# A two-layer hybrid encoder on one core: the second sequence's input normalised and transposed during the first one's attention, and the output projections with a tile of their own for the next layer's norm

## The chip, the core and the metric

One core of a Trainium2 chip. It has the engines PE (TensorE, matrix multiply and transpose), DVE (VectorE), ACT (ScalarE) and POOL (GpSimd); SP (SyncE) issues the DMAs of this kernel. Each engine executes its own instructions in the order in which the program gives them, and waits for the others through semaphores. The metric is device time in microseconds, lower is better.

## The reference, cut

Two sequences of 1024 tokens with 1024 features (`x_prompt` and `x_sample`) go through the same two layers. Layer 0 is attention (dilated windows and grouped queries), layer 1 is mean pooling over windows.

```python
h = _rmsnorm(x, pre_norm[l]) * (1.0 + scl) + shift   # shift, scl, gate: from c, by ada_w
if l % 2 == 0:
    m = _attn_mixer(h, attn_w_in[i], attn_q_norm[i], attn_k_norm[i], attn_w_out[i])
else:
    m = _pool_mixer(h, pool_w_in[i], pool_w_grp[i], pool_scale[i], pool_w_out[i])
x = x + gate * _rmsnorm(m, post_norm[l])
# in both mixers: (something of h @ w_in) * silu(gate part of h @ w_in), then @ w_out
```

## The kernel before, in words

Everything is fp32. A product is made of three matmuls: each operand is split into a high part and a low part that TensorE takes as fp32r, and high x high, high x low and low x high are added in PSUM. So three lines, such as L945 to L947, belong to one product.

`run` executes the stages for sequence s = 0 (prompt) and s = 1 (sample) in this order, with their places in the profiled span: `start` and `layer0(0)` (input and attention of the prompt, 0 to 800 us), `outproj0(0)` (output projection of layer 0, residual, and the norm of layer 1, 800 to 977), `layer0(1)` (to 1643), `outproj0(1)` (to 1798), `layer1(1)` (pooling layer of the sample, to about 2070), `layer1(0)` (to the end). The Python code writes instructions out in an order that interleaves generators by hand (`next(...)`), and a scheduler with a timeline of its own turns that into one fixed order for each engine. Tiles come from pools with so many buffers for each tag; an allocation waits until the oldest user of its buffer is done.

The places that the change touches:

- `outproj0`: eight tiles of 128 tokens. Tile i: `load(i)` brings the residual input `xt` (512 KB), PE makes the sums `S` (for the first two tiles they are made ahead of the stage, `pre`), ACT squares them for the post norm (L1061), POOL makes the reciprocal root (`rstd`, L123 to L125), DVE multiplies by the gate row (L1063) and adds the residual (L1064) in place in `xt`, and SP stores `xt` as x1 (`x_d<-xt`). Then `h_tile` makes the input of layer 1: ACT Square (L250), DVE scaling (L252) in place in `xt`, shift added by POOL (L253, for the last two tiles by DVE), eight PE transposes (L258), evacuation by ACT (L263) and, for the low part, DVE (L265). For s = 1 it goes to `hN`, in SBUF; for s = 0 to a stash in DRAM (`hs_d`), since layer 1 of the prompt is last.
- `outproj0(0)` does more: through the same `h_tile` it makes the layer-0 input of the second sequence from its raw input `xo` (`load_o`), tile by tile. `hq` is the queue of such generators, and `run_h` takes the next step of the oldest.
- `layer0`: attention. `adv(ui)` takes a step of unit ui of the input projection; for s = 0 and ui in 2, 3, 4 a part of the modulation (`ada_rest`) is made between such steps, at the steps listed in `marks`.
- `layer1(0)` begins by loading the stash and splitting it into high and low (L1083, L1084).
- `start` makes the layer-0 input of the first sequence in another form: scaling by the reciprocal root (L1299), transposes (L1304), and then scale and shift as an affine with a scalar for each partition (L1310 on ACT, L1311 on DVE), and the low part (L1312).

```python
            nc.vector.scalar_tensor_tensor(xt[i], jk, r, xt[i], op0=ALU.mult, op1=ALU.add)
            nc.sync.dma_start(x1o[i], xt[i])
            put = self.put_stash(op, i) if s == 0 else self.put_hT(hN, i)
            hq.append(self.h_tile(op, xt[i], g1, sh1, perm, put, jk, nc.vector if i >= NT - 2 else None))
```

The last line reuses `xt[i]`, which the store of the line before still reads.

Of the kernel before, what the change touches and what calls it, by code (L numbers as in the profile page):

```python
# [59 lines left out]
class Trunk:  # L60
    def __init__(self, ctx, tc, t):
# [28 lines left out]
        self.hs_d = self.dram.tile([NT, 2, P, 4, P], F32, name="hs_d")  # L90
# [73 lines left out]
    def ada_first(self, ap, stage):  # L164
# [4 lines left out]
        col = self.col = self.apool.tile([P, 2, 2, KT], F32, name="col")  # L169
# [75 lines left out]
    def h_tile(self, pool, x, g, sh, idm, put, junk=None, eng=None):  # L245
        nc = self.nc
        ss = pool.tile([P, 1], F32, name=self.n("ss"), tag="ss", bufs=6)
        if junk is None:
            junk = pool.tile([P, D], F32, name=self.n("jk"), tag="jk", bufs=2)
        nc.scalar.activation(junk, x, AF.Square, accum_out=ss)  # L250
        r = self.rstd(pool, ss, D, 1)
        nc.vector.scalar_tensor_tensor(x, x, r, g, op0=ALU.mult, op1=ALU.mult)  # L252
        (eng or nc.gpsimd).tensor_tensor(x, x, sh, ALU.add)  # L253
        for b in range(2):
# [6 lines left out]
            hi, lo, done = put(b)  # L261
            Tv = T.rearrange("p (k c) -> p k c", k=4)
            nc.scalar.activation(hi, Tv, AF.Copy)  # L263
            if lo is not None:
                nc.vector.tensor_tensor(lo, Tv, hi.bitcast(F32), ALU.subtract)  # L265
            if done:
                done()
            yield

    @staticmethod  # L270
    def put_hT(hT, i):
        def put(b):
            c = slice(i * P, (i + 1) * P)
            return hT[:, 4 * b : 4 * b + 4, 0, c], hT[:, 4 * b : 4 * b + 4, 1, c], None

        return put

    def put_stash(self, pool, i):
        def put(b):
            hl = pool.tile([P, 4, P], F32, name=self.n("hl"), tag="hl", bufs=2)  # L280
            return hl, None, lambda: self.nc.sync.dma_start(self.hs_d[i, b], hl)

        return put

# [288 lines left out]
    def layer0(self, s, hT, ap, side, after_proj, open2, run_h, first=None):  # L573
# [66 lines left out]
        rest = self.ada_rest(ap) if s == 0 else None  # L640
        started = {0, 1, 2}
# [3 lines left out]
        def adv(ui):  # L645
# [7 lines left out]
            if rest and ui in (2, 3, 4):  # L653
                if k in marks:
                    rest(k != marks[-1])
            if k == marks[-1] and ui + 1 < len(gens) and ui + 1 not in started:
                started.add(ui + 1)
                next(gens[ui + 1])
# [336 lines left out]
    def outproj0(self, s, wo, op, hN, pre, prefetch):  # L995
        nc, t = self.nc, self.t
        xsrc = (t["xp"] if s == 0 else t["xs"]).rearrange("(t m r) d -> t r m d", m=32, r=4)
        xos = t["xs"].rearrange("(hf p r) d -> r hf p d", hf=2, r=4)
        x1o = self.x1_d[s].rearrange("(t m r) d -> t r m d", m=32, r=4)
        hq = []  # L1000
        ys, xt, xo = {}, {}, {}

        def load(i):
            if i < NT:
                xt[i] = op.tile([P, D], F32, name=self.n("xt"), tag="xt", bufs=2)
                nc.sync.dma_start(xt[i], xsrc[i])
                if i >= 4:
                    ys[i] = []
# [539 lines left out]
```

## Time and profile before

| | |
|---|---|
| median of 3 runs | 2378.58 us (2374.77 to 2379.84) |
| the profiled execution: its span | 2374.5 us; no other time of that execution is given |
| PE busy | 2152.6 us, 91% |
| DVE busy | 1569.9 us, 66% |
| ACT busy | 1062.9 us, 45% |
| POOL busy | 1026.7 us, 43% |
| mean granted clock of TensorE | 0.957 |

The profile is of one execution, and its span lies within the three runs. Busy shares are averages over stages that differ; matmuls are pipelined, so a busy PE need not be at its peak. The granted clock is given as a share of full speed, 2.4 GHz; at the lower level, 1.2 GHz, a matmul takes twice the time.

### The profile page before, as it was taken

What the parts mean: (1) busy time and instruction counts of PE and PEld (TensorE: products, weight loads), DVE (VectorE), ACT (ScalarE), POOL (GpSimd) and SP (SyncE); (2) the same over time, 40 slices, a digit from 0 to 9 for tenths busy, and PEclk for the clock granted to TensorE, in tenths of its full rate; (3) what the DMA queues carried; (4) which work ended last, traced back from release to release, by engine and by line L of the source; (5) the groups of instructions that cost most, each with busy time, mean ns of one, the idle gap of its engine ahead of it and who ended that gap; (6) DMA issues with size and microseconds to landing.
All of it is one profiled execution on the core that took longest, in us unless ns stands there. A gap on an engine that the chain in (4) does not pass through costs nothing.

```text
span 2374.5 us, 38597 instructions
## 1 busy us (share of the span) xinstructions
PE 2152.6 (91%) x13777; PEld 1907.4 (80%) x13777; DVE 1569.9 (66%) x3453; ACT 1062.9 (45%) x2451; POOL 1026.7 (43%) x1455
## 2 busy tenths in 40 slices
PE   5999899999997866899999999988678999999998
PEld 3988788899997655898898999987457888778887
DVE  7788887767778344677878767775344454693536
ACT  6355555766665333355657666664221111310112
POOL 3675663135344253553321234433223345483552
PEclk9999999999997887999999999989789999999999
DMA  6123222112113444210011112124222111441113
GB/s 253 41 65 95 79 86 69 35 54 71 54 47 106 128 134 131 79 37 17 19 34 37 42 57 69 50 82 116 90 73 85 44 45 53 151 164 40 55 44 146
DMA packets 146561, 182.84 MB, mean 77 GB/s; under 512 B 13944, under 2 KB 109280, under 8 KB 146368
## 3 DMA queue, kind: packets, MB, share of 16 engines
q1 hardware_dynamic: 146032, 179.91, 24.1%
q8 instruction: 109, 1.79, 0.3%
q14 instruction: 84, 0.69, 0.1%
q10 hardware_dynamic: 144, 0.26, 0.0%
q0 software_dynamic: 192, 0.20, 0.0%
HBM read 142.33 MB, written 37.99 MB: 76 GB/s over the span
## 4 chain that ended last, share of the span: by engine, by line
PE 53%; DMA 15%; DVE 15%; issue 7%; POOL 6%; ACT 4%; SPq 0%; POOLq 0%; DVEq 0%; ACTq 0%
PE J L355 5%; PE J L357 5%; PE J L356 5%; PE S L1091 4%; PE S L1093 4%; PE S L1092 4%; DMA x_d<-xt 3%; PE H L676 3%; DMA xt<-xp 3%; POOL w L291 3%; PE T L714 2%; DVE E L694 2%; PE S L1186 2%; PE S L1188 2%; PE S L1187 2%
## 5 line engine op out<-in xcount | busy, mean ns | idle before, releaser
L291 POOL TENSOR_TENSOR w<-ws,w 128x256 fp32r<-128x256 f32 (+1 forms) x418 | 391.0, 949 | 360.0 <-DVE w L290 267.1
L355 PE MATMUL J<-w,hT 128*128 128x256 f32 x1664 | 482.5, 290 | 3.2 <-ACT xj L368 2.3
L357 PE MATMUL J<-w,hT 128*128 128x256 f32 x1664 | 477.5, 287 | 4.1 <-DVE hT L1312 3.9
L356 PE MATMUL J<-w,hT 128*128 128x256 f32 x1664 | 477.7, 287 | 0.4 <-POOL w L291 0.4
L355 PEld LDWEIGHTS J<-w,hT 128*128 128x128 f32 x1664 | 318.7, 192 | 7.2 <-ACT xj L368 3.7
L357 PEld LDWEIGHTS J<-w,hT 128*128 128x128 f32 x1664 | 318.5, 192 | 6.8 <-DVE hT L1312 4.6
L356 PEld LDWEIGHTS J<-w,hT 128*128 128x128 f32 x1664 | 318.5, 191 | 2.9 <-POOL w L291 0.9
L693 ACT ACTIVATE E<-T 128x512 fp32r<-128x512 f32 x384 | 226.8, 598 | 207.4 <-PE T L714 67.3
L694 DVE TENSOR_TENSOR E<-T,E 128x512 fp32r<-128x512 f32 x384 | 261.6, 682 | 84.5 <-ACT E L693 82.3
L290 DVE CAST w<-ws 128x256 fp32r<-128x256 f32 (+1 forms) x420 | 196.6, 493 | 169.5 <-PE S L1093 86.0
L683 ACT ACTIVATE P<-H,mx 128x512 f32<-128x512 f32 x256 | 173.7, 685 | 109.9 <-DVE mx L678 95.2
L1093 PE MATMUL S<-hT,w 128*128 128x512 f32 x512 | 200.5, 392 | 2.0 <-POOL w L291 2.0
L1091 PE MATMUL S<-hT,w 128*128 128x512 f32 x512 | 200.7, 392 | 0.0
L1092 PE MATMUL S<-hT,w 128*128 128x512 f32 x512 | 200.3, 391 | 0.0
L677 DVE TENSOR_REDUCE mx<-H 128x1 f32<-128x512 f32 x256 | 173.7, 681 | 34.1 <-PE H L676 32.0
L714 PE MATMUL T<-identr,P 128*128 128x128 f32 x1024 | 162.6, 274 | 6.9 <-DVE mr L151 3.2
L727 PE MATMUL O<-E,v 128*128 128x256 f32 x512 | 142.8, 301 | 14.1 <-DVE E L694 13.5
L793 ACT ACTIVATE P<-H,nm 128x256 f32<-128x256 f32 x256 | 117.7, 474 | 81.2 <-DVE nm L787 81.0
L726 PE MATMUL O<-E,v 128*128 128x256 f32 x512 | 146.1, 294 | 3.9 <-DVE X L748 2.2
L714 PEld LDWEIGHTS T<-identr,P 128*128 128x128 f32 x1024 | 122.4, 141 | 23.9 <-DVE mr L151 3.4
L441 POOL TENSOR_TENSOR hl<-xj,hl 128x256 fp32r<-128x256 f32 x64 | 48.2, 756 | 206.6 <-DVE hl L440 149.5
L727 PEld LDWEIGHTS O<-E,v 128*128 128x128 f32 x512 | 96.8, 189 | 27.2 <-DVE E L694 24.5
(264 smaller groups left out, 5228.8 us busy)
## 6 DMA issues: line engine op xcount, KB each, us to landing
ws<-win SPq DMA_DIRECT2D x192, 128.0 KB
ws<-ada_w SPq DMA_DIRECT2D x128, 128.0 KB
ws<-pwin SPq DMA_DIRECT2D x60, 256.0 KB
vb<-v_d SPq DMA_DIRECT2D x64, 144.0 KB
xt<-xp SPq DMA_DIRECT2D x16, 512.0 KB
ada<-ada_w SPq DMA_DIRECT2D x16, 512.0 KB
y_d<-X SPq DMA_DIRECT2D x32, 256.0 KB
v_d<-v SPq DMA_DIRECT2D x64, 128.0 KB
```

The costliest lines, as they stand in the source:

```text
L290: nc.vector.tensor_copy(hi, src)
L291: (nc.vector if dve_lo else nc.gpsimd).tensor_tensor(lo, src, hi.bitcast(F32), ALU.subtract)
L355: nc.tensor.matmul(ps, hi, w[:, 0, k, :], start=(k == 0), stop=False)
L356: nc.tensor.matmul(ps, hi, w[:, 1, k, :], start=False, stop=False)
L357: nc.tensor.matmul(ps, lo, w[:, 0, k, :], start=False, stop=(k == KT - 1))
L693: nc.scalar.activation(ov[0], Tv, AF.Copy)
L694: nc.vector.tensor_tensor(ov[1], Tv, ov[0].bitcast(F32), ALU.subtract)
L714: nc.tensor.transpose(T[:, (2 * e + i) * P : (2 * e + i + 1) * P], Pt[(h, 2 * g + i)][:, (2 * kp + e) * P : (2 * kp + e + 1) * P], self.ident)
L727: nc.tensor.matmul(O, st["v"][:, kk, :], pairs(ex, 1, e), start=False, stop=(kk == 7))
L1091: nc.tensor.matmul(ps[:, cs], w[:, 0, k, ws], hT[:, k, 0, cs], start=(k == 0), stop=False)
L1092: nc.tensor.matmul(ps[:, cs], w[:, 0, k, ws], hT[:, k, 1, cs], start=False, stop=False)
L1093: nc.tensor.matmul(ps[:, cs], w[:, 1, k, ws], hT[:, k, 0, cs], start=False, stop=(k == KT - 1))
```

## The change

The second sequence's layer-0 input is no longer made in `outproj0(0)`. A generator `x_ahead`, stepped in `layer0(0)` at the steps of units 2, 3 and 4 that are not marks, takes its eight raw tiles: load, Square and scaling by the reciprocal root, transposes, and a store of the transposed tile to a new DRAM tensor `xn_d`. In `outproj0(0)` a generator `h_affine` loads that by blocks of 128 features, and applies scale and shift as an affine. The stash `hs_d` of the first sequence likewise holds only the scaled and transposed tile, and `layer1(0)` applies its affine, with columns gathered from `mod_d`. In both `outproj0` the norm of the next layer is written into a tile of its own, `hx`, its transposes are put a tile later (`late`), and buffer counts change: `xt` 2 to 3, `jk` 1 to 2, `yh` 2 to 4, `y0` 2 to 3 for s = 0; the weight blocks fetched ahead for s = 1 have 2 buffers instead of 3. `h_tile` is divided into `normed` and `turned`.

```diff
         self.nc.sync.dma_start(r, self.mod_d[l, s, c : c + 1, :].to_broadcast([P, D]))
         return r
 
-    def h_tile(self, pool, x, g, sh, idm, put, junk=None, eng=None):
+    def normed(self, pool, x, out, junk, g=None, sh=None, eng=None):
         nc = self.nc
         ss = pool.tile([P, 1], F32, name=self.n("ss"), tag="ss", bufs=6)
-        if junk is None:
-            junk = pool.tile([P, D], F32, name=self.n("jk"), tag="jk", bufs=2)
         nc.scalar.activation(junk, x, AF.Square, accum_out=ss)
         r = self.rstd(pool, ss, D, 1)
-        nc.vector.scalar_tensor_tensor(x, x, r, g, op0=ALU.mult, op1=ALU.mult)
-        (eng or nc.gpsimd).tensor_tensor(x, x, sh, ALU.add)
+        if g is None:
+            nc.vector.tensor_scalar_mul(out, x, r)
+        else:
+            nc.vector.scalar_tensor_tensor(out, x, r, g, op0=ALU.mult, op1=ALU.mult)
+            (eng or nc.gpsimd).tensor_tensor(out, out, sh, ALU.add)
+
+    def turned(self, x, idm, put):
+        nc = self.nc
         for b in range(2):
             T = self.ptile("T")
             for k in range(4):
...
         E = ap.tile([P, 2 * ZB + 1, P], F32R, name=self.n("E"), tag="E", bufs=1)
         nc.gpsimd.memset(E[:, ZB, :].bitcast(F32), 0.0)
         rest = self.ada_rest(ap) if s == 0 else None
+        ahead = self.x_ahead(ap) if s == 0 else None
         started = {0, 1, 2}
         stepped = {}
         marks = [max(1, NSTEP * (i + 1) // 9) for i in range(7)]
...
             if rest and ui in (2, 3, 4):
                 if k in marks:
                     rest(k != marks[-1])
+                else:
+                    next(ahead, None)
+                    if k == NSTEP:
+                        next(ahead, None)
             if k == marks[-1] and ui + 1 < len(gens) and ui + 1 not in started:
                 started.add(ui + 1)
                 next(gens[ui + 1])
...
     def outproj0(self, s, wo, op, hN, pre, prefetch):
         nc, t = self.nc, self.t
         xsrc = (t["xp"] if s == 0 else t["xs"]).rearrange("(t m r) d -> t r m d", m=32, r=4)
-        xos = t["xs"].rearrange("(hf p r) d -> r hf p d", hf=2, r=4)
         x1o = self.x1_d[s].rearrange("(t m r) d -> t r m d", m=32, r=4)
-        hq = []
-        ys, xt, xo = {}, {}, {}
+        hq, late = [], []
+        ys, xt = {}, {}
 
         def load(i):
             if i < NT:
-                xt[i] = op.tile([P, D], F32, name=self.n("xt"), tag="xt", bufs=2)
+                xt[i] = op.tile([P, D], F32, name=self.n("xt"), tag="xt", bufs=3)
                 nc.sync.dma_start(xt[i], xsrc[i])
-                if i >= 4:
-                    ys[i] = []
-                    for f in range(2):
-                        y0 = op.tile([P, 4, P], F32, name=self.n("y0"), tag="y0", bufs=2)
-                        ys[i].append(op.tile([P, 2, 4, P], F32R, name=self.n("yh"), tag="yh", bufs=2))
-                        self.load_y(s, i, y0, ys[i][f], 4 * f, 4 * f + 4, 0)
-
-        def load_o(i):
-            if s == 0 and i < NT:
-                xo[i] = op.tile([P, D], F32, name=self.n("xo"), tag="xo", bufs=2)
-                nc.sync.dma_start(xo[i], xos[i // 2, i % 2])
+
+        def load_ys(i):
+            if 4 <= i < NT:
+                ys[i] = []
+                for f in range(2):
+                    y0 = op.tile([P, 4, P], F32, name=self.n("y0"), tag="y0", bufs=3 - s)
+                    ys[i].append(op.tile([P, 2, 4, P], F32R, name=self.n("yh"), tag="yh", bufs=4))
+                    self.load_y(s, i, y0, ys[i][f], 4 * f, 4 * f + 4, 0)
 
         def run_h(c):
             for _ in range(c):
...
                         run_h(1)
                         if i >= 4:
                             next(pf, None)
-            if s == 0:
-                jx = op.tile([P, D], F32, name=self.n("jx"), tag="jx", bufs=1)
-                hq.append(self.h_tile(op, xo[i], g0, sh0, self.ident, self.put_hT(hN, i), jx))
+            hq += late
+            hx = op.tile([P, D], F32, name=self.n("hx"), tag="hx", bufs=2)
             ss = op.tile([P, 1], F32, name=self.n("ss"), tag="ss", bufs=6)
-            jk = op.tile([P, D], F32, name=self.n("jk"), tag="jk", bufs=1)
-            nc.scalar.activation(jk, ps, AF.Square, accum_out=ss)
+            jk = op.tile([P, D], F32, name=self.n("jk"), tag="jk", bufs=2)
+            nc.scalar.activation(hx, ps, AF.Square, accum_out=ss)
+            nc.vector.tensor_tensor(jk, ps, pg, ALU.mult)
             r = self.rstd(op, ss, D, 1)
-            nc.vector.tensor_tensor(jk, ps, pg, ALU.mult)
             nc.vector.scalar_tensor_tensor(xt[i], jk, r, xt[i], op0=ALU.mult, op1=ALU.add)
             nc.sync.dma_start(x1o[i], xt[i])
-            put = self.put_stash(op, i) if s == 0 else self.put_hT(hN, i)
-            hq.append(self.h_tile(op, xt[i], g1, sh1, perm, put, jk, nc.vector if i >= NT - 2 else None))
+            self.normed(op, xt[i], hx, jk, g1, sh1, nc.vector if i >= NT - 2 else None)
+            put = self.put_stash(op, i, self.hs_d) if s == 0 else self.put_hT(hN, i)
+            late = [self.turned(hx, perm, put)]
+            if hN_of:
+                for _ in range(2):
+                    next(hN_of, None)
+        hq += late
         for _ in pf:
             pass
         return run_h
...
         kvw, self.kvw = self.kvw, None
         wu0 = kvw or self.l1_block(wp, t["pwin"][0])
         if s == 0:
-            for i in range(NT):
-                h = lp.tile([P, 2, 4, P], F32, name=self.n("h"), tag=("sg1", "wa")[i % 2], bufs=2)
-                for b in range(2):
-                    nc.sync.dma_start(h[:, b], self.hs_d[i, b])
-                    hi, lo = (hT[:, 4 * b : 4 * b + 4, e, i * P : i * P + P] for e in range(2))
-                    nc.scalar.activation(hi, h[:, b], AF.Copy)
-                    (nc.gpsimd if b and i % 2 else nc.vector).tensor_tensor(lo, h[:, b], hi.bitcast(F32), ALU.subtract)
+            hc = lp.tile([P, 2, KT], F32, name=self.n("hc"))
+            nc.sync.dma_start(hc, self.mod_d[1, 0, 0:2].rearrange("c (k p) -> p c k", p=P))
+            for _ in self.h_affine(lp, hT, self.hs_d, hc, ("sg1", "wa"), 2, 2):
+                pass
         outap = t["yp"] if s == 0 else t["ys"]
 
         def lin_c(ps, w, ct, c):
...
             def prefetch(sp):
                 self.wi = 0
                 out = []
-                yield from self.block_gen(None, sp, t["pwin"][0] if s else t["win"][8], out=out, bufs=1 if s == 0 else 3)
+                yield from self.block_gen(None, sp, t["pwin"][0] if s else t["win"][8], out=out, bufs=1 + s)
                 self.kvw = out[0]
 
             run_h = self.outproj0(s, after.wo, op, hT, pre, prefetch)
```

What the scheduler makes of it, at three places. First ACT, in the attention of the first sequence, around the Square of the third tile of `x_ahead`. `E` are evacuated transposes of the exponentials, `P` the exponentials (from scores `H` and maxima `mx`), `X` an evacuated output; `xa` is the raw tile, `xe` the tile that takes the squares and later the transposed halves. Before:

```order
L683 ACTIVATE P_2442,den_1925<-H_2432,mx_2434 128x512
L683 ACTIVATE P_2442,den_1925<-H_2433,mx_2434 128x512
L747 ACTIVATE X_2462<-O_2231 64x512
L693 ACTIVATE E_1302<-T_2471 128x2x256
L693 ACTIVATE E_1302<-T_2529 128x2x256
L683 ACTIVATE P_2526,den_1925<-H_2516,mx_2518 128x512
L683 ACTIVATE P_2526,den_1925<-H_2517,mx_2518 128x512
```

And with the change:

```order
L727 ACTIVATE P_2491,den_1950<-H_2481,mx_2483 128x512
L727 ACTIVATE P_2491,den_1950<-H_2482,mx_2483 128x512
L737 ACTIVATE E_1303<-T_2494 128x2x256
L791 ACTIVATE X_2511<-O_2266 64x512
L737 ACTIVATE E_1303<-T_2520 128x2x256
L249 ACTIVATE xe_2610,ss_2611<-xa_2560 128x1024
L737 ACTIVATE E_1303<-T_2580 128x2x256
L727 ACTIVATE P_2577,den_1950<-H_2567,mx_2569 128x512
L727 ACTIVATE P_2577,den_1950<-H_2568,mx_2569 128x512
```

The Square stands between the evacuation that follows `X` and the next one; the rest is as before.

Then SP, the queue that issues that tile's load. `ws` are blocks of weights, from the input projection (`win`) or the modulation (`ada_w`). Before:

```order
L306 DMA ws_2302<-win 128x256
L306 DMA ws_2306<-win 128x256
L306 DMA ws_2310<-win 128x256
L306 DMA ws_2314<-win 128x256
L306 DMA ws_2318<-win 128x256
L306 DMA ws_2322<-win 128x256
L157 DMA mod_d<-mr_2144 2x256
```

With the change:

```order
L345 DMA ws_2337<-win 128x256
L345 DMA ws_2341<-win 128x256
L285 DMA xn_d<-xe_2258 128x4x128
L345 DMA ws_2345<-win 128x256
L345 DMA ws_2349<-win 128x256
L294 DMA xa_2560<-xs 128x1024
L345 DMA ws_2353<-win 128x256
L345 DMA ws_2357<-win 128x256
L285 DMA xn_d<-xe_2258 128x4x128
L158 DMA mod_d<-mr_2171 2x256
```

The load of the tile and the two stores of the tile ahead of it stand among the weight loads, the load behind the fourth of them.

Last DVE, at the start of `outproj0(0)`. `row` are gate, scale and shift rows, `rr` reciprocal roots; `xo` is the raw input of the second sequence, `xk` a block of `xn_d`, `hT` the input that layer 0 of the second sequence reads. Before:

```order
L1063 TENSOR_TENSOR jk_10752<-S_10437,row_10729 128x1024
L1064 SCALAR_TENSOR_TENSOR xt_10731<-jk_10752,rr_10756,xt_10731 128x1024
L252 SCALAR_TENSOR_TENSOR xo_10735<-xo_10735,rr_10767,row_10737 128x1024
L1063 TENSOR_TENSOR jk_10811<-S_10603,row_10729 128x1024
L1064 SCALAR_TENSOR_TENSOR xt_10733<-jk_10811,rr_10815,xt_10733 128x1024
L252 SCALAR_TENSOR_TENSOR xo_10748<-xo_10748,rr_10841,row_10737 128x1024
L252 SCALAR_TENSOR_TENSOR xt_10731<-xt_10731,rr_10789,row_10743 128x1024
```

With the change:

```order
L1102 TENSOR_TENSOR jk_10939<-S_10630,row_10922 128x1024
L1104 SCALAR_TENSOR_TENSOR xt_10924<-jk_10939,rr_10944,xt_10924 128x1024
L252 TENSOR_SCALAR hx_10937<-xt_10924,rr_10952 128x1024
L1102 TENSOR_TENSOR jk_10969<-S_10796,row_10922 128x1024
L320 TENSOR_SCALAR xk_10929<-xk_10929,col 128x1024
L1104 SCALAR_TENSOR_TENSOR xt_10926<-jk_10969,rr_10974,xt_10926 128x1024
L320 TENSOR_SCALAR xk_10931<-xk_10931,col 128x1024
L321 TENSOR_TENSOR hT_10916<-xk_10929,hT_10916 128x1024
L320 TENSOR_SCALAR xk_10933<-xk_10933,col 128x1024
L282 COPY hl_11035<-T_11030 128x512
L321 TENSOR_TENSOR hT_10916<-xk_10933,hT_10916 128x1024
L320 TENSOR_SCALAR xk_10955<-xk_10955,col 128x1024
```

The scaling of the first tile (`hx`) now follows its multiply-add at once; the affines (L320) and low parts (L321) stand ahead of the scaling of the second tile, `L252 hx_10967`, which is the next row.

## Rows read from the trace of the kernel before

**Rows 1.** The page: its first line and the busy times.

```profile
span 2374.5 us, 38597 instructions
PE 2152.6 (91%) x13777; PEld 1907.4 (80%) x13777; DVE 1569.9 (66%) x3453; ACT 1062.9 (45%) x2451; POOL 1026.7 (43%) x1455
```

**Rows 2.** Windows: length, busy (instructions) of PE, PEld, DVE, ACT, POOL, clock, DMA, GB/s.

```profile
800.00:850.00 50.00, 38.73 (x167) 30.81 (x166) 17.66 (x20) 12.98 (x26) 20.63 (x21) 0.90 0.58 173
...
900.00:950.00 50.00, 31.35 (x130) 24.42 (x128) 21.25 (x21) 13.87 (x26) 20.70 (x24) 0.81 0.44 137
...
1700.00:1750.00 50.00, 33.47 (x123) 25.83 (x122) 22.99 (x26) 10.02 (x20) 19.50 (x23) 0.80 0.27 85
...
2050.00:2100.00 50.00, 49.35 (x214) 39.83 (x213) 47.08 (x36) 20.73 (x34) 37.80 (x31) 1.00 0.57 204
```

**Rows 3.** Waits, 800 to 975: total us, times, longest us.

```profile
DVE xt L252 <- DMA x_d<-xt: 51.4, 8, 8.6
...
ACT jx L250 <- DMA xo<-xs: 42.1, 5, 16.6
...
DVE xt L1064 <- DMA xt<-xp: 21.1, 5, 6.9
```

**Rows 4.** Waits, 1640 to 1800.

```profile
DVE xt L252 <- DMA x_d<-xt: 57.4, 8, 9.4
```

**Rows 5.** Chain that ended last, 780 to 1010: start us, us, what.

```profile
800.01 13.37 DMA xt<-xp
...
915.20 11.01 DMA x_d<-xt
...
976.91 0.44 PE T L258 x4
```

**Rows 6.** Chain that ended last, 1640 to 1800.

```profile
1644.40 17.83 DMA xt<-xs
...
1663.55 9.96 DMA x_d<-xt
...
1677.30 1.98 PE T L258 x8
1679.34 8.74 DMA xt<-xs
...
1798.15 1.05 PE S L1091 x2
```

**Rows 7.** Groups by line and shape, 800 to 975: busy us, mean ns | idle before.

```profile
L263 ACT ACTIVATE hl<-T 128x512 f32<-128x512 f32 x15 | 8.5, 591 | 22.0 <-PE T L258 21.1 <-ACT jk L250 0.9
...
L250 ACT ACTIVATE jx<-xo 128x1024 f32<-128x1024 f32 x8 | 8.4, 1053 | 42.1 <-DMA xo<-xs 42.1
```

**Rows 8.** Windows of 50 us in the first attention.

```profile
250.00:300.00 50.00, 43.35 (x304) 36.66 (x303) 46.11 (x106) 27.85 (x63) 33.01 (x49) 1.00 0.27 80
```

**Rows 9.** Timeline of ACT: start us, us, what, [idle before <-releaser].

```profile
200.47 0.60 ACT L693 ACTIVATE E<-T 128x512 fp32r<-128x512 f32 x1
202.78 0.60 ACT L693 ACTIVATE E<-T 128x512 fp32r<-128x512 f32 x1 [1.71 <-PE O L726]
204.63 0.69 ACT L683 ACTIVATE P<-H,mx 128x512 f32<-128x512 f32 x1 [1.25 <-PE T L714]
```

**Rows 10.** Timeline of SP, the DMA issues around 200 us.

```profile
195.22 6.95 SPq L306 DMA_DIRECT2D ws<-win  x6
```

**Rows 11.** Groups by line and shape, 2050 to 2130.

```profile
L1084 DVE TENSOR_TENSOR hT<-h,hT 128x512 fp32r<-128x512 f32 x10 | 12.8, 1306 | 0.0
...
L1084 POOL TENSOR_TENSOR hT<-h,hT 128x512 fp32r<-128x512 f32 x4 | 6.6, 1662 | 1.7 <-ACT hT L1083 1.7
```

**Rows 12.** Groups by line and shape of DVE, 0 to 115.

```profile
L1299 DVE TENSOR_SCALAR xt<-xt,rr 128x1024 f32<-128x1024 f32 x8 | 7.3, 918 | 10.0 <-POOL rr L125 9.9
...
L1312 DVE TENSOR_TENSOR hT<-xT,hT 128x512 fp32r<-128x512 f32 x10 | 6.8, 692 | 0.0
...
L1311 DVE TENSOR_SCALAR xT<-xT,col 128x512 f32<-128x512 f32 x8 | 6.0, 779 | 0.0
```

More of the change, by code (lines that the diff above doesn't have):

```diff
@@ L89, in __init__ @@
         self.y_d = self.dram.tile([2, D, S], F32, name="y_d")
-        self.hs_d = self.dram.tile([NT, 2, P, 4, P], F32, name="hs_d")
+        self.hs_d = self.dram.tile([KT, P, S], F32, name="hs_d")
+        self.xn_d = self.dram.tile([KT, P, S], F32, name="xn_d")
         self.v_d = [self.dram.tile([4, 288, P], F32, name=f"v_d{i}") for i in range(3)]
@@ L168, in ada_first @@
         nc.sync.dma_start(cst, t["adaT"])
-        col = self.col = self.apool.tile([P, 2, 2, KT], F32, name="col")
+        col = self.col = self.base.tile([P, 2, 2, KT], F32, name="col")
         hl = ap.tile([P, 2, 2, D], F32R, name="ahl", tag="w", bufs=1)
@@ L273, in put @@
             c = slice(i * P, (i + 1) * P)
-            return hT[:, 4 * b : 4 * b + 4, 0, c], hT[:, 4 * b : 4 * b + 4, 1, c], None
-        return put
[L278 to L281, printed above, removed]
-        return put
+            hi, lo = (hT[:, 4 * b : 4 * b + 4, e, c] for e in range(2))
+            self.nc.scalar.activation(hi, Tv, AF.Copy)
@@ new lines, in put, with put_stash @@
+            self.nc.vector.tensor_tensor(lo, Tv, hi.bitcast(F32), ALU.subtract)
+        return put
+    def put_stash(self, pool, i, dst, tag="hl", bufs=3, one=None):
+        def put(b, Tv):
+            hl = one[:, b] if one is not None else pool.tile([P, 4, P], F32, name=self.n("hl"), tag=tag, bufs=bufs)
+            if b:
+                self.nc.vector.tensor_copy(hl, Tv)
+            else:
+                self.nc.scalar.activation(hl, Tv, AF.Copy)
+            self.nc.sync.dma_start(dst[4 * b : 4 * b + 4, :, i * P : i * P + P].rearrange("k p c -> p k c"), hl)
+        return put
@@ new lines, in x_ahead @@
+    def x_ahead(self, ap):
+        nc = self.nc
+        xv = self.t["xs"].rearrange("(hf p r) d -> r hf p d", hf=2, r=4)
+        for i in range(NT):
+            x = ap.tile([P, D], F32, name=self.n("xa"), tag="vb", bufs=2)
+            nc.sync.dma_start(x, xv[i // 2, i % 2])
+            yield
+            xe = ap.tile([P, 2, 4, P], F32, name=self.n("xe"), tag="vb", bufs=2)
+            self.normed(ap, x, x, xe.rearrange("p b k c -> p (b k c)"))
+            yield
+            yield from self.turned(x, self.ident, self.put_stash(ap, i, self.xn_d, one=xe))
@@ new lines, in h_affine, with load @@
+    def h_affine(self, pool, hT, src, col, tags, bufs, ahead):
+        nc = self.nc
+        xk = []
+        def load():
+            k = len(xk)
+            if k < KT:
+                xk.append(pool.tile([P, S], F32, name=self.n("xk"), tag=tags[k % len(tags)], bufs=bufs))
+                nc.sync.dma_start(xk[k], src[k])
+        for _ in range(ahead):
+            load()
+        yield
+        for k in range(KT):
+            load()
+            x = xk[k]
+            hi, lo = (hT[:, k, e, :] for e in range(2))
+            g, sh = col[:, 1, k : k + 1], col[:, 0, k : k + 1]
+            nc.scalar.activation(hi, x, AF.Identity, scale=g, bias=sh)
+            nc.vector.tensor_scalar(x, x, g, sh, op0=ALU.mult, op1=ALU.add)
+            (nc.gpsimd if k % 2 else nc.vector).tensor_tensor(lo, x, hi.bitcast(F32), ALU.subtract)
+            yield
```

33 lines of the change are left out of this document (14 added, 19 removed).

## The prediction

> **What bounds the kernel now.** I read the page first: PE is busy 91% of the span [rows 1], so the kernel can only get much faster where PE is idle or granted a low clock. The windows of 50 us show where that is. In the pooling layer PE is busy 49.35 of 50 us at clock 1.00; in the two output projections (about 800 to 977 us and 1643 to 1798 us) it is busy 31 to 39 of 50, at a clock of 0.80 to 0.90 [rows 2]. Of the two levels, 1.2 and 2.4 GHz, the lower is granted there after PE has stood idle, so part of the busy time is itself lost time.
>
> Why does PE stand there? The waits of the first projection name three transfers [rows 3]: DVE waits for the store of x1 (51.4 us in 8 waits), since the next-layer norm overwrites the tile that the store still reads; ACT waits for the second sequence's input (42.1 us in 5); DVE waits for the residual input (21.1 us in 5). The second projection has only the first kind, 57.4 us in 8 [rows 4]. The chain of waits agrees: in both stages long pieces of DMA alternate with short pieces of DVE, and PE's transposes come at the end of each link [rows 5, 6].
>
> **How long the stages need be.** A matmul of 128x512 takes 49.35/214 = 0.231 us at full clock [rows 2]. A tile of the projection is 48 of them and 8 transposes, which go four in 0.44 us [rows 5]: 48 x 0.231 + 0.88 = 12.0 us.
>
> **First projection (edit: own norm tile, later transposes, second input taken ready from DRAM).** Before, from 800.0 to the last transpose at 976.9 + 0.4 = 977.3 us. After, the store of x1 holds nothing up, and the Square, multiply-add, shift and 64 transposes of the second input are gone from here; in their place stand eight loads of the same 512 KB and affines on ACT, DVE and POOL, of which DVE has some 8 us a tile against PE's 12. The first residual tile still has to land: 13.37 us [rows 5]; some 3 us more, an estimate, since three loads of normalised tiles are queued close to it, then multiply-add 1.3 us (1662.2 to 1663.5, [rows 6]) and norm scaling 0.9 [rows 12]; with the rstd between them and PE's own backlog the first transposes come near 823. The sums of the first two tiles are made ahead of the stage, so six tiles of 12.0 follow: 895. The tail (Square and multiply, rstd, multiply-add, scaling, transposes) is about 6, and the scalings of tiles 2 and 8 come late in DVE's queue, 4 us each, an estimate (in the order the scaling of tile 2 stands seven places behind its multiply-add, with three affines, two subtractions and a copy between). That gives 909, a gain of 68. I take off 13: each load of a residual tile now waits in SP's queue for a store that takes 11.01 us [rows 5] and was issued just ahead of it, and the stores of the stashed halves are queued behind that load, with three buffers for two halves a tile. **Gain 55.** Bounds: 83 with no stall (813.4 + 2.5 + 72 + 6 = 894); 35 if the stage stays as bound by transfers as it is: it issues some 20.3 MB where it issued 22.7 (DMA issues counted from the order), and at 143 GB/s, between the 137 and 173 of its windows [rows 2], 20.3 MB last 142 us.
>
> **Second projection (own norm tile, later transposes).** Before: first transposes at 1677.30, the first matmul of the next layer behind the last transposes at 1798.15 [rows 6], so seven tiles in 120.9 us, 17.3 each. After: the first residual load still takes 17.83 us from 1644.40 [rows 6], the multiply-add 1.3, norm and shift 3.8 (from the store's end at 1673.5 to 1677.3), some 2 us of reciprocal root stand between: transposes near 1670, as the 9.96 us of the store are gone. Six more tiles at 12.0: 1742, and a tail of 8 with the shift on DVE: 1750. 48 us, of which I take 46. Bounds 52 (no tail beyond the transposes' own) and 20 (the loads set the pace: a residual load alone took 8.74, with company 17.83 [rows 6]).
>
> **The work that is moved into the first attention.** Eight tiles are loaded, squared, scaled, transposed and stored in 150 to 400 us, where PE is busy 43 of 50 us even in the worst window, DVE 46 and ACT 28 [rows 8]. The work alone: PE 64 transposes x 0.11 = 7 us; ACT 8 x (1.05 + 0.59) = 13 us [rows 7], in an engine that is idle 22 of 50; DVE 8 x (0.92 + 0.69), the copy at the price of a subtraction of its size, = 13 us [rows 12]. In a PE-bound stretch PE's 7 count fully, the others hardly.
>
> The order shows the dear part. ACT executes in order, and the Square of a tile stands in ACT's queue almost where SP issues that tile's load. Take tile 3: SP issues it behind the fourth of the `ws<-win` loads, which in the trace of before is at 199 to 201 us [rows 10]; its Square stands behind one X and one E evacuation, the latter at 200.5 to 201.1 us [rows 9]. Tile 2 stands the same way, and so do tiles 4 to 8, to within 4 us; only tile 1 is loaded well ahead. A 512 KB load took 8.74 us where it had little beside it [rows 6]. The same instruction on the same tile waited 42.1 us in 5 waits, 8.4 each, in the first projection [rows 3]. So ACT will stand some 8.7 us seven times. Behind the Square wait the evacuations E and the exponentials P of the attention, and PE waits for those. ACT is not ahead of PE there: before each E it waits for PE for 1.71 and 1.25 us [rows 9], so PE has only that and the tiles in flight as cover: I allow 2.7 us. Loss 7 x (8.7 - 2.7) = 42, with the transposes 49, minus what PE's own gaps take up: **+48.** Bounds: 7 (every load lands ahead of its Square) and 113: 7 x 15 + 8, with loads as slow as 17.83 [rows 6], since SP also issues the weight blocks and a store of 512-byte pieces that the Square waits for.
>
> A rule speaks for less. The Trainium skill, "DMA: Bandwidth & Descriptors", section "Anatomy of one DMA", gives a transfer as 2.0 us and its bytes at 436 GB/s: 3.2 us for 512 KB, an estimate by that page. This trace disagrees by its 8.74 us; by the page ACT would wait 3.2 - 2.7 = 0.5 us a tile and the kernel would end as in rival 1.
>
> **Pooling layer of the first sequence.** Its input is now made by affines at the start of the stage, from 8 loads of 512 KB instead of 16 of half. DVE is busy 47.08 and POOL 37.80 of 50 us there [rows 2], and each slows the other: the subtraction of 128x512 takes DVE 1.306 us there [rows 11] and 0.692 in the quiet start [rows 12]. DVE: 8 affines of 128x1024 at 2 x 0.78 [rows 12] or 1.1 and 4 subtractions of 2 x 1.31, 19 to 23 us, for 12 x 1.31 = 16; POOL: 4 subtractions of 2 x 1.66 for 4 of 1.66 [rows 11], 7 us more. PE has no cover of its own there, but the first matmuls need only the first blocks. **+6**, bounds 0 and 15. The 4-byte gather of the two columns is issued some 300 us ahead and is hidden.
>
> **Sum.** -55 - 46 + 48 + 6 = -47. The profiled execution's span is 2374.5 us, so 2327.5; the median of the runs shown, 2378.58, is 4.1 above that span: **2332 us**.
>
> **Rivals.**
> 1. The attention hides the moved work: loads are issued earlier on the chip than the neighbours suggest, or land in 3 us. For it: ACT is idle 22 of 50 us [rows 8], and SP's weight loads wait only for buffers. Against it: 8.4 us a wait for the same tile [rows 3]. Then +10 for +48: 2294.
> 2. The projections stay bound by transfers: gains 35 and 20 by the bounds above. For it: the residual loads are the largest links of the first stage's chain already [rows 5]. Against it: three buffers for two, 2.4 MB less. With the attention's +48: 2377.
> 3. Slower: the same head-of-queue wait in ACT, at a higher price. At 113 in the attention it is -55 - 46 + 113 + 6 = +18, 2397. It decides from 95 us on, 12.6 us of PE for each Square. That asks for loads of some 15 us there; 17.83 has been seen with several transfers in flight [rows 6], while DMA share in the attention is 0.27 [rows 8], half that of the projection.
>
> **Chances.** The forecast 0.58 (its own range 2308 to 2355), rival 1 0.17, rival 2 0.10, rival 3 0.10, and 0.05 for lesser gains, 2355 to 2373. A measurement of this kernel can tell 0.2%, 5 us, from no change. Faster: 0.58 + 0.17 + 0.05 and a little of rival 2, 0.82; same 0.07, out of rival 2; slower 0.11. The range leaves out the lower part of rival 1 and all of rival 3: 2286 to 2376.
>
> **What would show it.** In the profile after: no wait of DVE for the x1 store in either stage, PE at 45 or more of 50 us with the clock above 0.9, tiles at 12 to 14 us; the first projection 50 to 65 us shorter, the second 40 to 50. In the attention: ACT waiting for the loads of `xa`, some 55 us in 7 waits, and the stage 40 to 60 us longer. In the last layer a few us more of PE idle in its first 80. I am wrong if ACT's wait for `xa` is below 20 us or above 90, or if DVE or the slots of the stash (`hl`) replace the store as the pace of the first projection.

## The result, and the profile after

The changed kernel takes 2352.32 us (median of 4 runs, 2346.7 to 2354.61) against 2376.82 for the kernel before: a ratio of 0.9887, 95% interval 0.9871 to 0.9902. The forecast was 2332 in a range of 2286 to 2376: the sign and the range held, the gain is about half of what was forecast. The profiled span is 2349.2 us.

Three places mark the stages in both traces: SP's first residual load of a projection, and the first and last transposes with the permutation (`T<-perm`). SP's timeline of the kernel after (start us, us):

```profile
817.02 1.32 SPq L1049 DMA_DIRECT2D xt<-xp  x2
...
1645.42 1.24 SPq L1049 DMA_DIRECT2D xt<-xs  x2
```

The view of the transposes' line after, for each projection (ns min/median/max, first and last start):

```profile
L263 PE MATMUL T<-perm,hx x64: 270/273/476, 836.3 to 957.4; 128*128 128x128 f32 x64
...
L263 PE MATMUL T<-perm,hx x64: 270/273/476, 1668.5 to 1772.8; 128*128 128x128 f32 x64
```

The same two views of the kernel before:

```profile
800.01 1.32 SPq L1006 DMA_DIRECT2D xt<-xp  x2
...
1643.69 1.27 SPq L1006 DMA_DIRECT2D xt<-xs  x2
```

```profile
L258 PE MATMUL T<-perm,xt x64: 270/273/476, 840.4 to 977.1; 128*128 128x128 f32 x64
...
L258 PE MATMUL T<-perm,xt x64: 271/418/477, 1677.3 to 1797.7; 128*128 128x128 f32 x64
```

Their differences are the ledger of the change, and of the experiments below (us; the last column is what remains to the end of the span):

| kernel | to the first load | 1st projection | second attention | 2nd projection | rest |
|---|---|---|---|---|---|
| before | 800.0 | 177.1 | 666.6 | 154.0 | 576.8 |
| after | 817.0 | 140.4 | 688.0 | 127.4 | 576.4 |
| difference | +17.0 | -36.7 | +21.4 | -26.6 | -0.4 |
| forecast | +48 | -55 | not named | -46 | +6 |

The ledger compares one profiled execution of each kernel. How far that holds, two of the experiments show: e5 turned out to be the change's own program and begins its first projection at 820.3 us for 817.0, and e12, which has the same order as the kernel before up to the second projection, at 804.5 for 800.0. So the +17.0 is 12 to 20; the other stages of these pairs agree within 1.4 us.

The page after, which answers to [rows 1], and then the windows, with the columns of [rows 2]. PE's share is 91% as before, with 12 us less of it. In the first projection PE is busier than the 31 of before, in the second only from 1700 us on (41 for 33; 33 for 35 in the window ahead of it), and in both it is far from 50 of 50.

```profile
span 2349.2 us, 38580 instructions
...
PE 2140.3 (91%) x13777; PEld 1904.1 (81%) x13777; DVE 1562.4 (67%) x3463; ACT 1065.3 (45%) x2435; POOL 1009.8 (43%) x1445
```

```profile
850.00:900.00 50.00, 35.51 (x149) 28.47 (x148) 20.82 (x25) 14.06 (x21) 15.77 (x16) 0.86 0.54 176
900.00:950.00 50.00, 36.99 (x173) 30.54 (x172) 14.18 (x21) 8.80 (x16) 9.79 (x17) 0.83 0.38 116
...
1650.00:1700.00 50.00, 33.42 (x126) 25.96 (x126) 19.30 (x18) 10.70 (x20) 10.47 (x13) 0.81 0.41 133
1700.00:1750.00 50.00, 41.13 (x163) 32.73 (x164) 22.08 (x28) 12.15 (x22) 19.11 (x26) 0.85 0.26 84
```

The waits in the first projection after (total us, times, longest). The store of x1, 51.4 us in [rows 3], is gone; in its place DVE waits for weight loads, and PE for the norm tile `hx` that stands behind them in DVE's queue:

```profile
DVE w L329 <- DMA ws<-win: 35.1, 7, 9.2
...
PE T L263 <- DVE hx L252: 21.4, 5, 6.9
...
DVE hl L282 <- DMA hs_d<-hl: 8.1, 1, 8.1
```

DVE's timeline shows it. The cast of a weight piece (L329) stands for 8.87 us, idle, ahead of the gate multiply and the multiply-add; the next `hx` starts only at 907.89, behind one more such cast:

```profile
887.52 0.75 DVE L252 TENSOR_SCALAR hx<-xt,rr 128x1024 f32<-128x1024 f32 x1 [0.44 <-POOL rr L126]
897.14 0.29 DVE L329 CAST w<-ws 128x256 fp32r<-128x256 f32 x1 [8.87 <-DMA ws<-win]
897.35 1.22 DVE L1102 TENSOR_TENSOR jk<-S,row 128x1024 f32<-128x1024 f32 x1
898.48 0.68 DVE L983 TENSOR_TENSOR yh<-y,yh 128x512 fp32r<-128x512 f32 x1
899.60 1.28 DVE L1104 SCALAR_TENSOR_TENSOR xt<-jk,rr,xt 128x1024 f32<-128x1024 f32 x1 [0.44 <-POOL rr L126]
905.85 0.29 DVE L329 CAST w<-ws 128x256 fp32r<-128x256 f32 x1 [4.96 <-DMA ws<-win]
907.89 0.75 DVE L252 TENSOR_SCALAR hx<-xt,rr 128x1024 f32<-128x1024 f32 x1 [1.74 <-POOL rr L126]
```

In the second projection it is the same, one step on (POOL adds the shift there), where [rows 4] had 57.4 us for the store:

```profile
PE T L263 <- POOL hx L255: 22.2, 5, 8.4
...
DVE w L329 <- DMA ws<-pwin: 20.9, 4, 8.9
```

In the first attention the feared wait is not there. ACT's waits ahead of the Squares (`xe`), of 8 loads:

```profile
ACT xe L249 <- DMA xn_d<-xe: 5.3, 3, 2.1
...
ACT xe L249 <- DMA xa<-xs: 2.7, 1, 2.7
```

SP issues the first load at 87.35 and ACT goes on at 91.01, 3.66 us later; the third is issued at 201.01, and its Square at 206.64 waits for nothing. The Square stands farther behind its load than the order had suggested, by 4.95 to 5.70 us in tiles 2 to 8, and the load was done by then. SP's timeline, then ACT's:

```profile
87.35 0.33 SPq L294 DMA_DIRECT2D xa<-xs  x1
...
201.01 0.33 SPq L294 DMA_DIRECT2D xa<-xs  x1
```

```profile
91.01 1.06 ACT L249 ACTIVATE xe<-xa 128x1024 f32<-128x1024 f32 x1 [2.69 <-DMA xa<-xs]
...
206.64 1.06 ACT L249 ACTIVATE xe<-xa 128x1024 f32<-128x1024 f32 x1
```

The load of 8.74 us, from which the prediction took the price [rows 6], can be set beside the first load of `xa`. Both are 512 KB, and each was nearly alone. First the DMA view of the kernel before from 1678 to 1690 us, then of the kernel after from 85 to 92, in 40 slices each: the busy share of the 16 DMA engines in tenths, and GB/s.

```profile
DMA  1111110004201222222223223222110000000000
GB/s 43 38 44 43 43 44 5 0 0 82 27 27 82 109 109 68 68 109 68 82 82 96 82 96 109 96 96 82 68 68 27 14 0 0 0 0 0 0 0 0
```

```profile
DMA  0000000000000000000968299899610000000000
GB/s 0 0 0 0 0 0 0 0 0 0 0 0 0 0 0 0 0 0 23 187 117 164 117 398 468 351 421 374 258 70 23 23 0 0 0 0 0 0 0 0
```

The slow load has three tenths of the engines' time or less in all slices but one, the fast one eight or nine in most. In the code they differ in the order of their rows: four groups of 32 for `xt` (`t r m d`), one group of 128 for `xa` (`r hf p d`).

Last the second attention, +21.4 in the ledger. Its body is no slower: from the first score matmul (`H`, first and last start in each line) at 1012.3 us to the one at 1609.6 it takes 597.3 us before, and 597.1 after. Before, then after:

```profile
L676 PE MATMUL H<-kh,qT x128: 388/470/503, 1012.3 to 1314.4; 128*128 128x512 f32 x128
...
L765 PE MATMUL H<-kh,qT x64: 277/281/562, 1314.9 to 1609.6; 128*128 128x256 f32 x64
```

```profile
L720 PE MATMUL H<-kh,qT x128: 388/468/503, 1002.7 to 1305.6; 128*128 128x512 f32 x128
...
L809 PE MATMUL H<-kh,qT x64: 277/280/562, 1306.1 to 1599.8; 128*128 128x256 f32 x64
```

So 10.1 us were lost ahead of it and 11.5 behind it. A part of both is that the marks cut the work elsewhere: 38 more matmuls of the attention's input projection (`J`) and 19 more of the output projection's sums (`S`) fall between them. PE's windows between the marks (length, busy, instructions, clock, DMA share, GB/s), for `J` before and after:

```profile
977.10:1643.69 666.59, 335.25 (x2369) 0.98 0.17 48
957.40:1645.42 688.02, 340.50 (x2407) 0.97 0.17 49
```

For `S`, before and after:

```profile
977.10:1643.69 666.59, 19.82 (x77) 0.98 0.17 48
957.40:1645.42 688.02, 24.26 (x96) 0.97 0.17 49
```

That is some 10 us of PE's busy time (5.3 and 4.4) that before belonged to the projections, and their gains of 36.7 and 26.6 contain it.

### The profile page after: what moved, and what is told of

The parts are those of the page before. It is cut to its first block, busy times and chain, and to the rows that moved or that the text cites. A ratio compares the mean times of both kernels' runs of the same rounds, so it can differ in the third digit from the quotient of the medians.

```text
span 2349.2 us, 38580 instructions
## 1 busy us (share of the span) xinstructions
PE 2140.3 (91%) x13777; PEld 1904.1 (81%) x13777; DVE 1562.4 (67%) x3463; ACT 1065.3 (45%) x2435; POOL 1009.8 (43%) x1445
## 4 chain that ended last, share of the span: by engine, by line
PE 41%; DVE 7%; DMA 4%; ACT 3%; issue 2%; POOL 2%; SPq 1%; POOLq 0%; DVEq 0%; ACTq 0%
PE S L1135 5%; PE S L1134 5%; PE S L1133 5%; PE J L394 3%; PE J L396 3%; PE J L395 3%; PE S L1228 2%; PE S L1229 2%; PE S L1230 2%; PE H L720 2%; PE T L758 1%; DVE E L738 1%; DVE mx L721 1%; PE O L771 1%; DMA x_d<-xt 1%
## 5 line engine op out<-in xcount | busy, mean ns | idle before, releaser
L329 DVE CAST w<-ws 128x256 fp32r<-128x256 f32 (+1 forms) x420 | 186.9, 468 | 214.4 <-PE S L1135 77.9
## 6 DMA issues: line engine op xcount, KB each, us to landing
ws<-win SPq DMA_DIRECT2D x192, 128.0 KB
ws<-ada_w SPq DMA_DIRECT2D x128, 128.0 KB
v_d<-v SPq DMA_DIRECT2D x64, 128.0 KB
```

## The experiments

Each was timed against the kernel before; medians, and the ratio to before with its 95% interval. The stages are those of the ledger.

| run | us | ratio | to 1st load | 1st proj. | 2nd att. | 2nd proj. |
|---|---|---|---|---|---|---|
| change | 2352.3 | 0.9887 (0.9871 to 0.9902) | 817.0 | 140.4 | 688.0 | 127.4 |
| e1_ahead_only | 2398.5 | 1.0081 (1.0066 to 1.0096) | 816.2 | 181.2 | 672.1 | 149.8 |
| e2_nolate | 2350.8 | 0.9878 (0.9864 to 0.9893) | 817.3 | 141.6 | 685.4 | 128.4 |
| e3_inplace | 2389.6 | 1.0041 (1.0026 to 1.0056) | 819.2 | 161.4 | 683.2 | 147.3 |
| e4_xt4 | 2357.0 | 0.9901 (0.9883 to 0.9919) | 818.6 | 141.2 | 686.2 | 132.9 |
| e5_nopf | 2353.0 | 0.9897 (0.9880 to 0.9915) | 820.3 | 140.3 | 688.3 | 126.8 |
| e6_stact | 2359.8 | 0.9935 (0.9913 to 0.9957) | 815.7 | 143.4 | 687.1 | 131.5 |
| e7_l1plain | 2345.5 | 0.9868 (0.9852 to 0.9884) | 816.3 | 141.5 | 686.8 | 128.0 |
| e8_ahead_norm | 2375.6 | 0.9985 (0.9976 to 0.9995) | 803.0 | 175.9 | 664.2 | 150.6 |
| e9_wsnone | 2325.0 | 0.9770 (0.9752 to 0.9787) | 815.1 | 131.9 | 685.4 | 112.4 |
| e10_ws4 | 2339.9 | 0.9832 (0.9813 to 0.9851) | 818.1 | 133.4 | 685.5 | 124.7 |
| e11_ws4_act | 2339.5 | 0.9836 (0.9809 to 0.9864) | 817.9 | 133.2 | 686.1 | 124.6 |
| e12_own1 | 2355.3 | 0.9894 (0.9877 to 0.9911) | 804.5 | 178.4 | 665.3 | 128.5 |

**What the moved work costs (e1, e8).** The kernel before, with `x_ahead` added and its result unused; in e8 without transposes, copies and stores.

```diff
+        ahead = self.x_ahead(ap) if s == 0 else None
...
+                else:
+                    next(ahead, None)
```

> The kernel before, with only the moved work added to the first attention: eight tiles loaded, squared, scaled, transposed and stored to DRAM, where nothing reads them; both projections as before, so the second input is made twice. What it tells is the price of the moved work by itself. The prediction's step (ACT stands 8.7 us behind seven loads): 48 us, 2377 + 48 = 2425. The theory after reading the trace (loads landed in some 4 us, PE lost only its own 64 transposes and a few us of ACT waits): 15 us, 2392. A rival, that part of those 15 us belongs to the changed buffers and not to the work: under 8, below 2385.

> The kernel before with only a part of the moved work in the first attention: the eight tiles are loaded, squared and scaled, but not transposed, copied out or stored. Against the whole moved work (20 us over before, 2398): if the price is what PE itself executes (64 transposes) and what hangs on them, 5 to 8 us are left, 2384 to 2387; if it is ACT's standing behind loads, and DVE's scaling, 12 us or more are left, 2391 and above.

e1: the first projection begins 16.2 us later, the change's own 17.0; the total is 20 us worse, where 15 had been expected. So the price is the work's, not the buffers', and a third of the forecast's 48. e8: it begins 3.0 us later, within the 4.5 us of e12 and the kernel before, and the total is not longer at all (2375.6 for 2378.7), which neither expectation had. Loads, Squares and scalings are all but free there; most of the 16 us belong to transposes, evacuations and stores. PE's own 64 transposes, 7 us in the prediction, are about half of that; the rest was not taken apart.

**Own tile or later transposes (e2, e3).** The two halves of the edit to the projections, each undone.

```diff
-            late = [self.turned(hx, perm, put)]
+            hq.append(self.turned(hx, perm, put))
```

```diff
-            self.normed(op, xt[i], hx, jk, g1, sh1, nc.vector if i >= NT - 2 else None)
+            self.normed(op, xt[i], xt[i], jk, g1, sh1, nc.vector if i >= NT - 2 else None)
...
-            late = [self.turned(hx, perm, put)]
+            late = [self.turned(xt[i], perm, put)]
```

> The changed kernel, its transposes put into the queue at once instead of a tile later; own tile and moved input stay. If the later place is what keeps PE from standing behind the norm chain (about 4 us for each of 14 tiles): 40 us or more slower than the change, 2392 and above. If the scheduler finds much the same place anyway, or the transfers set the pace: within 8 us of 2352.

> The changed kernel, the norm of the next layer written over the residual tile again, as before the change, which the x1 store still reads; later transposes and moved input stay. If the own tile is what shortened the projections: DVE waits again some 50 us for the store in each, and 20 to 40 us come back, 2372 to 2392. If the later transposes hide that wait: under 8 us, below 2360.

The place in the code is worth nothing: the scheduler puts the transposes much where they were, the first and the last of each projection within 1.6 us. The own tile is worth 21.0 us in the first projection and 19.9 in the second. Without it the change is slower than the kernel it came from, by 0.3 to 0.6%, and the old wait is back. From e3's waits in the second projection:

```profile
DVE xt L254 <- DMA x_d<-xt: 51.9, 8, 8.2
```

**SP's queue (e4, e6).** Four residual buffers for three in the second projection (one `yh` less); and the stores of x1 issued by ACT.

```diff
-                xt[i] = op.tile([P, D], F32, name=self.n("xt"), tag="xt", bufs=3)
+                xt[i] = op.tile([P, D], F32, name=self.n("xt"), tag="xt", bufs=3 + s)
...
-                    ys[i].append(op.tile([P, 2, 4, P], F32R, name=self.n("yh"), tag="yh", bufs=4))
+                    ys[i].append(op.tile([P, 2, 4, P], F32R, name=self.n("yh"), tag="yh", bufs=4 - s))
```

```diff
-            nc.sync.dma_start(x1o[i], xt[i])
+            nc.scalar.dma_start(x1o[i], xt[i])
```

> The changed kernel, in the second projection four buffers for the residual tile instead of three, and three for the split output tiles instead of four, for the space. Theory of SP's queue: there SP waits 29 us in 5 times for the x1 store of three tiles ago before it may issue the next residual load, and the output tiles and weight blocks queued behind come late (ACT waits 26 us for them, DVE 21 us): 8 to 15 us faster, 2337 to 2344. Rival, the transfers' own time sets the pace, or the missing output buffer takes the place: within 4 us of 2352, or slower.

> The changed kernel, the stores of x1 issued by ACT instead of SP. SP then no longer stands until DVE has made the tile (15 us in 5 waits in the second projection, 8 in 2 in the first) and goes on with loads; ACT would wait for the same multiply-add anyway, since its next Square reads it. If SP's order is what holds the loads back: 6 to 15 us faster, 2337 to 2346. If it is the landing of the stores and loads: within 4 us of 2352. If the issue on ACT costs more than it frees: slower.

Neither is faster, against both theories; the second projection is 5.5 and 4.1 us longer. But neither took away the longest of SP's waits, that of a residual load for a store to land: 29.1 us in the change, 24.4 in e4 and 34.3 in e6. SP's waits in the second projection of e6:

```profile
SPq L1049 <- DMA x_d<-xt: 34.3, 3, 14.7
```

So e6 shows only that SP's waits for DVE are not the price; its wait for landings stays untried.

**The head of DVE's queue (e5, e9, e10).** First the weight piece moved behind the last tile in the code; then made from a row that lies in SBUF; then with more buffers.

```diff
-                        if i >= 4:
-                            next(pf, None)
```

```diff
-out=out, bufs=1 + s)
+out=out, bufs=1 + s, raw=[self.pgv] * 2)
```

```diff
-out=out, bufs=1 + s)
+out=out, bufs=6 if s else 4)
...
-                    y0 = op.tile([P, 4, P], F32, name=self.n("y0"), tag="y0", bufs=3 - s)
-                    ys[i].append(op.tile([P, 2, 4, P], F32R, name=self.n("yh"), tag="yh", bufs=4))
+                    y0 = op.tile([P, 4, P], F32, name=self.n("y0"), tag="y0", bufs=2)
+                    ys[i].append(op.tile([P, 2, 4, P], F32R, name=self.n("yh"), tag="yh", bufs=4 - s))
```

> The changed kernel, the weight block for the next stage no longer fetched between the products of tiles 4 to 7 but after the last tile. Theory of the queues' heads: DVE waits 35 us in the first projection and 21 us in the second for those weight loads, with the norm and the residual queued behind, so the last transposes of each projection come 10 us or more sooner (957 and 1772 us in the profile of the change), and the weights cost that or more behind it. Rival, the residual tiles, stores and output tiles set the pace without the weights: the last transposes move by less than 4 us. The total: 2340 to 2365 by the first, 2355 to 2370 by the second.

> The changed kernel, the weight block that is prepared inside each projection made from the gate row, which lies in SBUF, instead of from loaded weights: the same casts and subtractions on DVE and POOL, no loads to wait for (the key and value weights of the second sequence, and the first input weights of the pooling layer, are thus wrong). Theory, the head of DVE's queue: in the trace of the change DVE stands 35 us in 7 waits for these loads in the first projection and 21 us in 4 in the second, with the next-layer norm behind them, for which PE waits 21 us (DVE) and 22 us (POOL, one step on). Then each projection gets 10 to 20 us shorter, 2312 to 2332. Rival, the transfers of residual, x1 and output tiles set the pace: under 5 us each, above 2342.

> The changed kernel with more buffers for that weight block's pieces, 4 for 1 in the first projection and 6 for 2 in the second, paid for with one output tile buffer in each. The loads are then issued several tiles sooner, and the result stays the reference's. If DVE's waits for them are the price: 8 us or more faster in all, below 2344. If the loads are late for another reason (SP's queue, the rate of the transfers), or the output tiles now come late: within 5 us of 2352, or slower.

e5 tells nothing about the wait: the scheduler made of it the change's own program, the same instructions in the same order on every engine. It is a repetition of the change, 2353.0 us for 2352.3. From the waits of its first projection:

```profile
DVE w L329 <- DMA ws<-win: 34.9, 7, 9.4
```

e9 tells more: it is 27 us faster than the change, 8.5 in the first projection and 15.0 in the second. PE's wait for the norm tile goes down from 22.2 us to 6.4 in the second and from 21.4 to 13.2 in the first. The second then takes 112.4 us, near the 108 that the forecast's gain of 46 leaves of 154.0. But with the waits e9 takes away the transfers too, 1 MB of weight pieces in the second projection. e10 leaves nothing out and gets 12 us of the 27. DVE's waits in its first projection:

```profile
DVE w L329 <- DMA ws<-win: 7.8, 1, 7.8
```

The wait is down from 35.1 us and that stage is 7.0 us shorter: there the wait is most of the price, and not the traffic. In the second, where DVE still waits 23 us for its pieces, e10 gets only 2.7, so how much of e9's 15.0 is the wait and how much the traffic is not shown.

**The affine in the last layer (e7, e11).** Left out; then made by ACT instead of DVE (with e10's buffers).

```diff
-            nc.scalar.activation(hi, x, AF.Identity, scale=g, bias=sh)
-            nc.vector.tensor_scalar(x, x, g, sh, op0=ALU.mult, op1=ALU.add)
+            nc.scalar.activation(x, x, AF.Identity, scale=g, bias=sh)
+            nc.scalar.activation(hi, x, AF.Copy)
```

> The changed kernel without the affine (scale and shift) of the first sequence's last layer: its input is split straight from the stash, so that sequence's output lacks scale and shift there. Takes away 8 DVE instructions of 128x1024 in the stretch where the trace after lost 5 to 7 us. If those are the price: 4 to 7 us faster, 2345 to 2348. If the price lies in the eight loads of 512 KB, or in the subtractions of twice the size on POOL: within 3 us of 2352.

> e10 (more buffers for the weight pieces), and in the last layer of the first sequence the affine made once by ACT, in place, and its high part copied from that by ACT too, instead of by ACT and by DVE: 8 instructions of 128x1024 less on DVE in the stretch where DVE and POOL are both busy, 8 more on ACT, which is idle most of it. The result stays the reference's. If DVE is what is short there, most of the 5 us that leaving the affine out gave is kept: 4 us faster than e10, near 2336. If ACT's two passes put the first block's high part later than DVE's work did: no gain, 2340 or above.

Without the affine the span is 5.3 us shorter (2343.9 for 2349.2), with the projections as in the change: that is the price which the +6 stood for. Moved to ACT it gains nothing over e10 (2339.5 for 2339.9). In its trace POOL's subtraction waits 13.1 us for ACT's high part there; in the change it waited 22.3 us for DVE's affine. Why no time came of that stays open.

**One thing of the change alone (e12).** The kernel before, with only the second projection's norm in a tile of its own.

```diff
-        nc.vector.scalar_tensor_tensor(x, x, r, g, op0=ALU.mult, op1=ALU.mult)
+        if out is None:
+            out = x
+        nc.vector.scalar_tensor_tensor(out, x, r, g, op0=ALU.mult, op1=ALU.mult)
+        x = out
...
+            hx = op.tile([P, D], F32, name=self.n("hx"), tag="hx", bufs=2) if s else None
```

> The kernel before with one thing of the change: in the second projection the next-layer norm goes into a tile of its own (two buffers). Nothing is moved into the attention, the first projection and the last layer are as before. If the x1 store that the tile waited for (57 us of DVE's waits) is the price there, and if the later transposes and the buffer counts are not needed: the 20 us that writing in place cost the changed kernel in this stage are gained, 2356 to 2362. If the gain needs the third residual buffer or the later transposes: under 8 us, above 2370.

2355.3 us: these few lines give nearly what the whole change gives (2352.3). The second projection takes 128.5 us with them, 127.4 in the change. The own tile in both projections, without the move, was not tried.

## Why the prediction was right, and which of its terms were not

The sum held by luck, by errors that cancel: the loss in the attention was put 31 us too high, the gains of the projections 38 us too high, and a loss of 21 was not named. By two of its own signs of being wrong the prediction was wrong: ACT's wait for `xa` is 2.7 us where below 20 was the limit, and DVE, behind its casts, took the store's place in the first projection. PE at 45 of 50 us with a clock above 0.9 did not come either.

1. **The attention, +48, measured +17.0.** The step that failed is "So ACT will stand some 8.7 us seven times": ACT stood 2.7 us for one load and 5.3 for stores of the tile ahead. Both of its grounds fell. The Square does not stand where SP issues the load, but 4.95 to 5.70 us behind it, so that even a load of 8.74 us would have cost some 3 us a tile (8.74 less 5.70 or 4.95, an estimate). And the load of 8.74 us is of another kind: with no company it ran at two or three tenths of the DMA engines, while the loads of `xa` took under 3.7 us in tile 1 and at most 5.7 in the others. The order of the rows is what the two differ in; that it is the cause is not shown, since no run changed it alone. The rule that the prediction set aside is given by the Trainium skill, "DMA: Bandwidth & Descriptors", "Anatomy of one DMA", for transfers that GpSimd issues, and these are issued by SP; its 3.2 us for 512 KB, an estimate by that page, agrees with the first tile's 3.66 us from issue to use. Rival 1 had this part nearly right (+10), but not the rest.
2. **The first projection, -55, measured -36.7.** The store's wait went as said, and e3 shows 21.0 us to be its price. The step that failed is "six tiles of 12.0 follow": PE was not what set the pace. The list of what would prove this wrong named the store's successor as DVE or the stash; it was DVE, by casts that wait for weights (7.0 us by e10, 8.5 by e9). The rest of the shortfall of 18.3 is in waits for the tiles `xk` and `y` and a lower clock (0.83 to 0.93), not separated here.
3. **The second projection, -46, measured -26.6.** Same step; e9, without the loads of the weight pieces, gives 15.0 us of the 19.4 missing. The prediction named no wait for these loads in the projections, though the chain before showed `ws<-pwin` there (14.85 us from 1712.15 on). A rival stays untested in both projections: the residual loads and the stores of x1 have the same order of rows as the load of 8.74 us. A load and a store in flight together, from 1691 to 1703 us of the kernel before, had a DMA share of 0.24 and 79 GB/s; at that rate the 8.4 MB of eight loads and eight stores last 106 us, an estimate, and no run changed them.
4. **The last layer, +6.** Mechanism and size right by e7 (5.3 us). From the first high part of that layer (L1083 before, L319 after) to the end it is 333.2 us for 330.5; the pooling layer ahead, from the last transposes on, is 243.2 for 246.3, so the rest of the span is unchanged. Why that got shorter stays open.
5. **The second attention, not named, +21.4.** All kernels that take the input from `xn_d` show 683 to 688 us here, those that make it in the projection 664 to 672. Some 10 us are the work that lies on the other side of the marks. At the start a copy of the stash waits 8.1 us for a store, with the attention's first DVE work behind it. What causes the rest, at the end of the stage, stays open.
6. **Chances.** Rival 2 (the projections stay bound by transfers) was given 0.10 and had half the truth: its gains of 35 and 20 are nearer to 36.7 and 26.6 than the forecast's 55 and 46. In the first projection it was in part the place at which DVE waits, not the bytes: e10 has them all and takes 133.4 us, less than the 142 of the bound.

## What to carry to other kernels

When a wait is taken off an in-order engine, read the rest of that engine's queue in the same stage: any other instruction that waits for a late load is the next head, here a small cast that stood in front of the norm. A tile of its own for a value that overwrites a tile still being stored is cheap and gave nearly the whole gain; a large move that only makes room for it should be priced alone (e3, e12). And a transfer's duration is read from a transfer with the same order of rows, not only of the same size.

## What the runs showed of the hardware

Two loads of 512 KB that were nearly alone differed by more than two times: 8.74 us from issue to landing at up to 109 GB/s (`xt`, four groups of 32 rows), and under 3.7 us at up to 468 GB/s (`xa`, one group of 128 rows). Loads of `xa` that had weight loads beside them, at a DMA share of 0.49 (195 to 210 us), still landed in under 5.7 us. So neither the size nor the share of a stretch alone tells how long a transfer takes. The order written in the code had no effect in e2 and e5: in e5 the scheduler made the very same order, in e2 much the same; buffer counts did (e10).
